# Modulation panels of the feed-forward layers in three places of their own, loaded by GpSimd's queue

## The chip, the cores and the metric

The kernel runs on one core of a Trainium2 chip. Five engines work beside each other, each through its own list of instructions, in order: TensorE (PE in the profile, its weight loads PEld), VectorE (DVE), ScalarE (ACT), GpSimd (POOL) and SyncE (SP), which here issues every DMA. The metric is the device time of one execution in microseconds; the median of three runs of the kernel before is 2368.94 us.

## The reference, cut to what matters

A transformer of two blocks, each of two layers, over 512 tokens of width 1024 in float32. The change touches the two layers of the first block:

```python
c_act = jax.nn.silu(c)
for l in range(DEPTH):                          # 2 layers
    mod = c_act @ ada_w[l] + ada_b[l]           # 1024 -> 6144
    sh1, sc1, g1, sh2, sc2, g2 = split(mod, 6)
    h = x * (1.0 + sc1) + sh1
    y = _even_mixer(h, ...) if l % 2 == 0 else _pool_mixer(h, ...)
    x = _layer_norm(ALPHA * x + g1 * y, ...)
    h = x * (1.0 + sc2) + sh2
    y = _conv_ffn(h, ...)                       # 1024 -> 2 x 2816 -> 1024
    x = _layer_norm(ALPHA * x + g2 * y, ...)
# the second block: mod = silu(c_2) @ ada_w_2[l] + ada_b_2[l], 1024 -> 3072, and the same for c_ctx_2
...
def _conv_ffn(h, w_up, conv_w, conv_b, w_down):
    u, v = jnp.split(h @ w_up, 2, axis=-1)
    ...                                         # causal convolution of width 3 over the tokens of u
    return (jax.nn.silu(uc) * v) @ w_down
```

The modulation vectors are products of one condition vector with a large matrix, so there is much weight to load and little to compute: 96 panels for the first block, and 48 for the second, whose panels serve two condition vectors each.

## The kernel before

**Weights.** A weight panel holds the weights of 128 output columns: 128 partitions by up to 1024 float32. `panel_load` (L342) brings it by DMA into a tile `ws`; `panel_split` turns it into a high part `wh` on ScalarE (L321) and a remainder `wl` on VectorE (L333). TensorE makes three products of a panel and an input that was split in the same way (`mm3`, L356 to L358). In the first block `ws` has four places (`stage=4`) and `wh` and `wl` three each (`panels=3`).

**The feed-forward layer** (`ffn`). It runs in two parts. Each part has 22 up tiles of 24 matmuls each, then 8 down tiles of 33 matmuls each, over the 11 hidden tiles of that part. An up tile that carries u goes through the convolution (a copy with bias on ScalarE, two L981 on VectorE, silu on ScalarE); one that carries v is multiplied in (L987), and the product is split into `gh` (L321) and `gl` (L333), which the down tiles read. A down tile is added to x with its gate (L993 in the first part, L605 in the second).

**Modulation panels.** `ada` makes a list of pieces. A piece loads one panel of 128 rows by 1024 into a `ws` tile (L437) and lets VectorE multiply it with the condition vector, which is held in every partition, and sum along the row (L440): one column of the modulation. For the second block's vectors there are two such instructions for each panel; the first of them writes its product to a scratch tile `ada`. The last piece of a list also loads the bias into a `ws` tile (L444) and adds it (L447). So panels of both kinds take the same four `ws` places in turn, and all loads stand in SyncE's queue.

**When pieces are called.** Lists stand in `self.pending`. `project` calls one piece after each up tile (`background(1)`) and two after each down tile (`bg=DBG`, 2); `flush` calls the rest of a list where its results are needed. In the first feed-forward layer these are list "d" (40 pieces, layer 1) and list "f" (24 pieces with two instructions each, second block); in the second they are "e" (8 pieces) and "g" (24 pieces with two instructions each). The panels of layer 0 are done before the first feed-forward layer.

**Order.** The program text does not fix the order of an engine's instructions. When the program is built, a planner puts them in an order, by its own reckoning of when inputs and places are there; on the chip each engine then keeps that order, and waits where an input is late. `tile(..., tag, bufs)` gives a tile one of `bufs` places in turn; a load waits until the last reader of that place is done. GpSimd has work in the layer norms (`x` in L521), and in the pooling layer between the two feed-forward layers (L1043; L1027 clears pads there).

Of the kernel before, what the change touches and what calls it, by code (L numbers as in the profile page):

```python
# [10 lines left out]
F32 = mybir.dt.float32  # L11
# [6 lines left out]
P = 128  # L18
# [63 lines left out]
def _vector_columns():  # L82
    at, n = {}, 0
    for name, size in _VEC_SIZES:
        at[name] = n
        n += size // P
    return at, n
# [185 lines left out]
class Program:  # L273
    def __init__(self, ctx, tc, I, C, out):
        self.ctx, self.tc, self.nc, self.I, self.C, self.out = ctx, tc, tc.nc, I, C, out
        pool = lambda name, **k: ctx.enter_context(tc.tile_pool(name=name, bufs=1, **k))
        self.keep, self.acts = pool("keep"), pool("acts")
        self.table_users = []
        self.pin(PIN[0])
        self.at, self.nvec = _vector_columns()  # L280
        self.pending = []

    def pools(self, ctx, name, psum, panels=4, stage=4, pk=8):

# [139 lines left out]
    def ada(self, src, cact, bias, dst, tiles, key):  # L424

        nc = self.nc

        class Piece:
            def __init__(self, f):
                self.f, self.key = f, key  # L430

            def __call__(self):
                self.f()

        def piece(m):
            ws = self.wp.tile([P, 1024], F32, tag="ws", name="ws", bufs=self.sbufs)
            nc.sync.dma_start(out=ws, in_=src[m])  # L437
            for i, (c, d) in enumerate(zip(cact, dst)):
                w = self.cp.tile([P, 1024], F32, tag="ada", name="ada") if i < len(dst) - 1 else ws
                nc.vector.scalar_tensor_tensor(out=w, in0=ws, scalar=1.0, in1=c, op0=ALU.mult, op1=ALU.mult, accum_out=d[:, m:m + 1])  # L440

        def close():
            b = self.wp.tile([P, 1024], F32, tag="ws", name="ws", bufs=self.sbufs)
            nc.sync.dma_start(out=b[:, :bias.shape[-1]], in_=bias)  # L444
            for d in dst:
                for a, n in runs:
                    nc.vector.tensor_tensor(out=d[:, a:a + n], in0=d[:, a:a + n], in1=b[:, a:a + n], op=ALU.add)  # L447

        tiles = list(tiles)
        runs = []  # L450
        for m in sorted(tiles):
            if runs and sum(runs[-1]) == m:
                runs[-1] = (runs[-1][0], runs[-1][1] + 1)
            else:
                runs.append((m, 1))
        work = [Piece(lambda m=m: piece(m)) for m in tiles]
        if key == "a":
            return work
        return work[:-1] + [Piece(lambda: (piece(tiles[-1]), close()))]


# [148 lines left out]
    def block1_even(self):  # L610
# [4 lines left out]
        lead, pan = list(range(16, 22)), []  # L615
        pss = [self.psum(("acc0", "sw")[q > 3]) for q in range(6)]
        first = ada(0, [c for m in range(8) for c in (8 + m, m)], "a")
        b = self.keep.tile([P, 48], F32, name="ada_b0")
        with tc.tile_pool(name="e1", bufs=1) as ep:
# [4 lines left out]
            for k in range(KT):  # L624
# [16 lines left out]
                if k == 1:  # L641
                    self.constants()
            self.pending += ada(0, range(16, 24), "b") + ada(0, range(24, 40), "b2") + ada(0, range(40, 48), "c")
            k_lev = self.const("k_levels", ep, I32)
            k_reset = self.const("k_reset", ep)
# [321 lines left out]
    def ffn(self, l, hh, hl, beside=None):  # L967
        nc, tc = self.nc, self.tc
        st = self.stats()
        half = NFF // 2  # L970
        with tc.tile_pool(name=f"ffn{l}", bufs=1) as fp:
            cw = lambda j, f: self.vec("conv_w", (3 * l + j) * NFF + f)
            held, gh, gl = {}, [], []

            def evac(m, ps):
                f = m // 2
                if m % 2 == 0:
                    a = fp.tile([P, T], F32, tag="a", name="a", bufs=2)
                    self.act(a, ps, AF.Identity, scale=cw(2, f), bias=self.vec("conv_b", l * NFF + f))
                    for j in (1, 2):  # L980
                        nc.vector.scalar_tensor_tensor(  # L981
                            out=a[:, j:], in0=ps[:, :T - j], scalar=cw(2 - j, f), in1=a[:, j:], op0=ALU.mult, op1=ALU.add)
                    self.act(a, a, AF.Silu)
                    held[f] = a
                else:
                    a = held.pop(f)
                    nc.vector.tensor_tensor(out=a, in0=ps, in1=a, op=ALU.mult)  # L987
                    for t, g in (("gh", gh), ("gl", gl)):
                        g.append(fp.tile([P, T], F32R, tag=t, name=t, bufs=GBUFS))
                    self.split(gh[-1], gl[-1], a)  # L990

            def first(m, ps):
                nc.vector.scalar_tensor_tensor(out=self.x[:, m, :], in0=ps, scalar=self.mod(l, 5)[:, m:m + 1], in1=self.x[:, m, :],  # L993
                                               op0=ALU.mult, op1=ALU.add)

            def second(m, ps):
                self.residual(st, l, 5, m, ps)
                if m == KT // 2 and beside:
                    beside()

            for part in range(2):
                self.project(self.I[f"up{l}"], list(range(2 * half * part, 2 * half * (part + 1))), KT, [(hh, hl, T)], evac, lead=3 if part == 0 else 1)
                if part == 0:
                    self.flush("c" if l == 0 else "e")
                    self.finish_gate(l, 5)
                self.project(self.I[f"down{l}"], list(range(KT)), half, [(gh, gl, T)], second if part else first, lead=1,
                             k_at=half * part, chunk=(half + 1) // 2, bg=DBG)
                gh.clear()
                gl.clear()
        return st  # L1010


# [68 lines left out]
    def block1_layers(self):  # L1081
        ada = lambda l, ch, key: self.ada(self.I["ada"][l], self.cact[:1], self.I["ada_b"][:, 48 * l:48 * l + 48], [self.mods[l]], ch, key)
        hh, hl = self.block1_even()
        self.pool_share = 0
        self.cond_open()
        self.pending += ada(1, range(40), "d") + self.ada2(0, "f")
        sums = self.ffn(0, hh, hl, self.context)
        self.flush("f")
        hh, hl = self.h_tiles()
        feed = self.context_feed(0, CTX_TILES[0])  # L1090
        self.weave([self.block1_odd(sums, hh, hl)], feed, CRATE[0])
        feed.finish()
        self.pending += ada(1, range(40, 48), "e") + self.ada2(1, "g")
        sums = self.ffn(1, hh, hl)
        self.flush("g")
        return self.between(sums)
# [1113 lines left out]
```

## Time and profile before

| | |
|---|---|
| runs | 2364.86, 2368.94, 2371.18 us (median 2368.94) |
| profiled execution | 2364.25 us, of which the span of the trace is 2362.4 us; granted clock of TensorE 0.976 of full speed |
| PE busy | 2213.0 us, 94% of the span |
| DVE busy | 1632.0 us, 69% |
| ACT busy | 1131.2 us, 48% |
| POOL busy | 354.7 us, 15% |
| DMA | 269.64 MB, all of the kernel's own issues by SP; 37.4% of 16 engines' span |
| L440, both kinds | 192 instructions, 180.2 and 58.7 us busy; DVE idle before them 84.4 and 29.8 us |

The span runs from the first instruction of the trace to the last; the execution's own time has a little more around it. Busy is the time in which an engine works on an instruction; waits and DMA issues are not counted. The first feed-forward layer lies at about 300 to 661 us of the span, the pooling layer after it at about 661 to 760 us, and the second feed-forward layer at about 760 to 1129 us. In rows of the timeline the bracket gives the engine's idle time before the instruction and what ended it; `x3` counts instructions merged into a row. In rows of windows each engine has its busy time and, in brackets, its count of instructions; then stand the granted clock, the busy share of the 16 DMA engines and GB/s.

### The profile page before, as it was taken

Reading aid. Unit: us, or ns where it says so; the run is one execution under the profiler, and the core shown is the slowest. Engines: PE = TensorE matmul, PEld = TensorE weight load, DVE = VectorE, ACT = ScalarE, POOL = GpSimd, SP = SyncE. Lnnn points to the kernel's source line nnn. Section 1 sums busy time; section 2 is a strip of 40 time slices with the busy share of each in tenths; the row PEclk is TensorE's granted clock in tenths of the full one; section 3 lists DMA queues with packets and bytes.
Section 4 is the critical chain, followed back from the end, with each engine's and each line's share of the span. In section 5 each row is a group of like instructions: output and inputs, shape, how many; then the busy total and the mean of one; then the engine's idle time right before and its main releaser. Section 6 shows DMA issues by size and latency. Waiting matters only on the chain.

```text
span 2362.4 us, 39796 instructions
## 1 busy us (share of the span) xinstructions
PE 2213.0 (94%) x15486; PEld 1784.4 (76%) x15486; DVE 1632.0 (69%) x3032; ACT 1131.2 (48%) x2105; POOL 354.7 (15%) x728
## 2 busy tenths in 40 slices
PE   6989989999998999999898999999999999999996
PEld 4667768778775787888686777777787777888885
DVE  6799886578859687444676787787776646555544
ACT  3466453223344332333564565656555445655542
POOL 1321020000002000000103433342423100000001
PEclk9999999999999999999999999999999999999998
DMA  8433456566624656323322222222212432422221
GB/s 285 140 127 125 135 158 194 177 212 195 191 70 139 200 178 205 105 85 97 135 74 60 47 58 53 59 47 60 62 45 46 129 129 92 138 72 72 63 63 45
DMA packets 203933, 269.64 MB, mean 114 GB/s; under 512 B 125408, under 2 KB 137568, under 8 KB 203360
## 3 DMA queue, kind: packets, MB, share of 16 engines
q1 hardware_dynamic: 203744, 267.09, 37.4%
q8 instruction: 122, 2.00, 0.3%
q14 instruction: 67, 0.55, 0.1%
HBM read 250.38 MB, written 16.66 MB: 113 GB/s over the span
## 4 chain that ended last, share of the span: by engine, by line
PE 68%; DVE 15%; DMA 7%; ACT 4%; issue 3%; POOL 2%; SPq 0%; DVEq 0%; ACTq 0%; POOLq 0%
PE acc L358 14%; PE acc L356 14%; PE acc L357 14%; DMA ws<-in_ada_dram 5%; PE c L1751 3%; DVE wl L333 2%; DVE ws L440 2%; PE acc L369 1%; PE sp L1646 1%; PE acc L370 1%; PE sp L1836 1%; PE acc L368 1%; PE misc L1854 1%; PE u L1815 1%; PE u L1646 1%
## 5 line engine op out<-in xcount | busy, mean ns | idle before, releaser
L356 PE MATMUL acc<-hh,wh 128*128 128x512 f32 x1416 | 573.5, 406 | 35.0 <-ACT wh L321 18.3
L358 PE MATMUL acc<-hh,wl 128*128 128x512 f32 x1416 | 570.0, 403 | 11.4 <-DVE wl L333 6.7
L357 PE MATMUL acc<-hl,wh 128*128 128x512 f32 x1416 | 571.4, 404 | 2.0 <-DVE hl L333 1.9
L321 ACT ACTIVATE wh<-ws 128x1024 fp32r<-128x1024 f32 (+3 forms) x307 | 275.5, 901 | 405.9 <-PE acc L357 302.8
L333 DVE TENSOR_TENSOR wl<-ws,wh 128x1024 fp32r<-128x1024 f32 (+4 forms) x294 | 304.8, 1040 | 189.2 <-ACT wh L321 186.5
L356 PEld LDWEIGHTS acc<-hh,wh 128*128 128x128 f32 x1416 | 269.5, 190 | 94.6 <-ACT wh L321 20.1
L358 PEld LDWEIGHTS acc<-hh,wl 128*128 128x128 f32 x1416 | 269.2, 190 | 77.4 <-DVE wl L333 12.4
L357 PEld LDWEIGHTS acc<-hl,wh 128*128 128x128 f32 x1416 | 269.8, 191 | 59.4 <-issue 6.1
L440 DVE SCALAR_TENSOR_TENSOR ws<-ws,cact 128x1024 f32<-128x1024 f32 x144 | 180.2, 1253 | 84.4 <-DMA ws<-in_ada_dram 83.5
L356 PE MATMUL acc<-gh,wh 128*128 128x512 f32 x352 | 138.4, 393 | 4.0 <-ACT gh L321 4.0
L1671 POOL TENSOR_TENSOR sO<-sN,sX 64x15 f32<-64x15 f32 (+2 forms) x270 | 87.3, 323 | 355.8 <-DMA sN<-lt 336.1
L358 PE MATMUL acc<-gh,wl 128*128 128x512 f32 x352 | 138.2, 393 | 1.5 <-DVE wl L333 1.4
L357 PE MATMUL acc<-gl,wh 128*128 128x512 f32 x352 | 138.2, 393 | 0.9 <-DVE gl L333 0.9
L321 ACT ACTIVATE a<-a 128x512 f32<-128x512 f32 x44 | 27.8, 633 | 203.8 <-DVE a L981 203.5
L1672 POOL TENSOR_TENSOR sX<-sX,sO 64x15 f32<-64x15 f32 (+2 forms) x270 | 89.3, 331 | 21.2
L1844 DVE SCALAR_TENSOR_TENSOR S<-sp,gc,gs 64x64 f32<-64x64 f32 x240 | 57.9, 280 | 36.4 <-PE sp L1836 32.7
L2013 POOL TENSOR_TENSOR raw<-raw,k_axial 128x512 f32<-128x512 f32 x16 | 21.9, 1366 | 399.3 <-ACT raw L321 209.7
L356 PEld LDWEIGHTS acc<-gh,wh 128*128 128x128 f32 x352 | 66.5, 189 | 18.9 <-ACT gh L321 5.2
L358 PEld LDWEIGHTS acc<-gh,wl 128*128 128x128 f32 x352 | 66.6, 189 | 16.9 <-DVE wl L333 3.2
L440 DVE SCALAR_TENSOR_TENSOR ada<-ws,cact 128x1024 f32<-128x1024 f32 x48 | 58.7, 1222 | 29.8 <-DMA ws<-in_ada_dram 29.8
L357 PEld LDWEIGHTS acc<-gl,wh 128*128 128x128 f32 x352 | 66.5, 189 | 15.6 <-DVE gl L333 1.9
L356 PE MATMUL acc<-hc,wh 128*128 128x256 f32 x208 | 64.3, 309 | 8.7 <-issue 3.7
(583 smaller groups left out, 4505.3 us busy)
## 6 DMA issues: line engine op xcount, KB each, us to landing
ws<-in_ada_dram SPq DMA_DIRECT2D x144, 512.0 KB, 4.3
ws<-in_up_dram SPq DMA_DIRECT2D x88, 512.0 KB, 4.0
ws<-in_od_in_dram SPq DMA_DIRECT2D x44, 512.0 KB, 3.5
ws<-in_ev_in_dram SPq DMA_DIRECT2D x60, 256.0 KB, 2.9
ws<-in_down_dram SPq DMA_DIRECT2D x32, 384.0 KB, 3.2
ws<-in_w_in_dram SPq DMA_DIRECT2D x22, 512.0 KB, 4.6
ws<-in_down_dram SPq DMA_DIRECT2D x32, 320.0 KB, 3.0
ws<-in_ev_in_dram SPq DMA_DIRECT2D x18, 512.0 KB, 3.6
```

The lines of the kernel that those rows point to most:

```text
L321: ins = self.nc.scalar.activation(out=out, in_=in_, func=func, **k)
L333: (engine or self.nc.vector).tensor_tensor(out=lo, in0=x, in1=hi.bitcast(F32), op=ALU.subtract)
L356: nc.tensor.matmul(ps, wh[:, s], xh, start=start, stop=False)
L357: nc.tensor.matmul(ps, wh[:, s], xl, start=False, stop=False)
L358: nc.tensor.matmul(ps, wl[:, s], xh, start=False, stop=stop)
L368: nc.tensor.matmul(out, xh[:, k, t], wh, start=(k == 0), stop=False)
L440: nc.vector.scalar_tensor_tensor(out=w, in0=ws, scalar=1.0, in1=c, op0=ALU.mult, op1=ALU.mult, accum_out=d[:, m:m + 1])
L1646: nc.tensor.matmul(ps[:, j, :], self.BZ[:, d, h, j, :], st["AR"][d][:, j // 2, i:i + 2, :].rearrange("p s t -> p (s t)"), start=True, stop ...
L1671: pt(out=ob, in0=N[:, :j, j:j + 1].to_broadcast(sh), in1=X[:, j:j + 1, j:].to_broadcast(sh), op=ALU.mult)
L1672: pt(out=X[:, :j, j:], in0=X[:, :j, j:], in1=ob, op=ALU.subtract)
L1751: nc.tensor.matmul(ps[64 * i + r0:64 * i + r0 + m, x, :], lhs(x, i), rhs(x, i), start=True, stop=True)
L1844: nc.vector.scalar_tensor_tensor(out=nxt[H, d, H], in0=sp[H, d], scalar=gd, in1=gs[H, d, H], op0=ALU.mult, op1=ALU.add)
```

## The change

Within `ffn`, from its start to its end, pieces of modulation no longer take `ws` places and SyncE's queue: their panels and biases go to tiles `wa` with three places in the layer's own pool (12 KB more in each partition), and GpSimd's queue issues their loads. That holds for the 96 pieces of lists d, f, e and g and their four biases, 100 loads. Elsewhere `ada_place` is empty and pieces are staged as before.

```diff
-        self.pending = []
+        self.pending, self.ada_place = [], None
...
+        def staged(n, ap):
+
+            pool, tag, bufs, eng = self.ada_place or (self.wp, "ws", self.sbufs, nc.sync)
+            t = pool.tile([P, 1024], F32, tag=tag, name=tag, bufs=bufs)
+            eng.dma_start(out=t[:, :n], in_=ap)
+            return t
+
         def piece(m):
-            ws = self.wp.tile([P, 1024], F32, tag="ws", name="ws", bufs=self.sbufs)
-            nc.sync.dma_start(out=ws, in_=src[m])
+            ws = staged(1024, src[m])
...
         def close():
-            b = self.wp.tile([P, 1024], F32, tag="ws", name="ws", bufs=self.sbufs)
-            nc.sync.dma_start(out=b[:, :bias.shape[-1]], in_=bias)
+            b = staged(bias.shape[-1], bias)
...
     def ffn(self, l, hh, hl, beside=None):
...
             held, gh, gl = {}, [], []
+            self.ada_place = fp, "wa", 3, nc.gpsimd
...
                 gh.clear()
                 gl.clear()
+            self.ada_place = None
         return st
```

## Rows read from the trace of the kernel before

**Rows 1.** The page, part 4: shares of the chain that ended last, by line.
```profile
PE acc L358 14%; PE acc L356 14%; PE acc L357 14%; DMA ws<-in_ada_dram 5%; PE c L1751 3%; DVE wl L333 2%; DVE ws L440 2%; PE acc L369 1%; PE sp L1646 1%; PE acc L370 1%; PE sp L1836 1%; PE acc L368 1%; PE misc L1854 1%; PE u L1815 1%; PE u L1646 1%
```

**Rows 2.** Windows over stretches of both feed-forward layers; columns as told above.
```profile
326.00:434.00 108.00, 107.63 (x476) 88.81 (x475) 72.99 (x100) 39.93 (x52) 0.00 (x0) 1.00 0.62 194
434.00:498.00 64.00, 61.27 (x264) 48.94 (x263) 37.66 (x57) 14.04 (x18) 0.00 (x0) 1.00 0.64 208
498.00:621.00 123.00, 122.34 (x537) 100.03 (x536) 105.22 (x163) 40.34 (x54) 0.00 (x0) 1.00 0.61 192
621.00:661.00 40.00, 37.75 (x159) 30.56 (x158) 27.37 (x44) 15.03 (x25) 0.00 (x0) 0.96 0.57 181
879.00:941.00 62.00, 60.55 (x267) 49.60 (x266) 49.90 (x79) 15.46 (x21) 0.00 (x0) 1.00 0.62 205
941.00:1062.00 121.00, 121.00 (x536) 100.25 (x535) 56.36 (x65) 43.13 (x53) 0.00 (x0) 1.00 0.32 96
```

**Rows 3.** Waits of PE, 330 to 661 us: total, times, longest.
```profile
PE acc L356 <- ACT gh L321: 2.8, 2, 1.9
PE acc L358 <- DVE wl L333: 2.3, 5, 0.9
PE acc L357 <- DVE gl L333: 0.6, 2, 0.3
```

**Rows 4.** Waits of PE, 760 to 1129 us.
```profile
PE acc L356 <- ACT gh L321: 1.2, 1, 1.2
```

**Rows 5.** Groups of DVE, 330 to 661 us: busy, mean ns | idle before.
```profile
L440 DVE SCALAR_TENSOR_TENSOR ws<-ws,cact 128x1024 f32<-128x1024 f32 x61 | 74.6, 1222 | 56.7 <-DMA ws<-in_ada_dram 56.4
...
L440 DVE SCALAR_TENSOR_TENSOR ada<-ws,cact 128x1024 f32<-128x1024 f32 x24 | 29.3, 1222 | 13.4 <-DMA ws<-in_ada_dram 13.4
```

**Rows 6.** Timeline of DVE, 621 to 630 us.
```profile
623.48 1.22 DVE L440 SCALAR_TENSOR_TENSOR ada<-ws,cact 128x1024 f32<-128x1024 f32 x1 [1.33 <-DMA ws<-in_ada_dram]
...
625.90 1.22 DVE L440 SCALAR_TENSOR_TENSOR ada<-ws,cact 128x1024 f32<-128x1024 f32 x1
...
627.04 0.69 DVE L987 TENSOR_TENSOR a<-acc,a 128x512 f32<-128x512 f32 x1
```

**Rows 7.** Timeline of PE, start of the second part's down tiles.
```profile
628.45 0.49 PE L356 MATMUL acc<-gh,wh 128*128 128x512 f32 x1 [1.94 <-ACT gh L321]
...
630.20 0.63 PE L357 MATMUL acc<-gl,wh 128*128 128x512 f32 x1
```

**Rows 8.** Windows: the two stretches with the most DMA.
```profile
0.00:59.00 59.00, 36.66 (x130) 25.90 (x131) 38.84 (x76) 22.10 (x27) 9.46 (x8) 1.00 0.82 285
...
626.00:636.00 10.00, 7.75 (x27) 5.69 (x26) 7.30 (x12) 5.08 (x13) 0.00 (x0) 0.83 0.81 280
```

**Rows 9.** Timeline of SP: the first load of list d.
```profile
295.80 0.33 SPq L437 DMA_DIRECT2D ws<-in_ada_dram  x1
```

**Rows 10.** Groups of POOL, 300 to 761 us.
```profile
L521 POOL TENSOR_SCALAR x<-t,pcol 128x512 f32<-128x512 f32 x16 | 28.9, 1816 | 96.4 <-DVE t L515 95.6 <-ACT cm L321 0.7
...
L1027 POOL MEMSET ph<- 128x16 f32 x4 | 0.2, 111 | 362.8 <-PE acc L358 362.8
```

**Rows 11.** Timeline of DVE after the last piece of list d.
```profile
507.75 0.20 DVE L447 TENSOR_TENSOR mods<-mods,ws 128x40 f32<-128x40 f32 x1
...
508.36 0.16 DVE L1021 TENSOR_TENSOR gs<-mods,pcol 128x8 f32<-128x8 f32 x1
```

**Rows 12.** L440 from 296 to 330 us: ns min/median/max, first and last start.
```profile
L440 DVE SCALAR_TENSOR_TENSOR ws<-ws,cact x3: 1226/1625/1629, 321.4 to 326.8; 128x1024 f32<-128x1024 f32 x3
```

**Rows 13.** DMA issues, 326 to 661 us: count, KB, median us to landing.
```profile
ws<-in_ada_dram SPq DMA_DIRECT2D x61, 512.0 KB, 4.3
...
hh<-in_ctx_dram SPq DMA_DIRECT2D x1, 1024.0 KB, 5.8
```

**Rows 14.** Window over the end of the pooling layer.
```profile
700.00:760.00 60.00, 48.28 (x166) 31.54 (x166) 56.85 (x104) 29.18 (x47) 20.20 (x13) 0.91 0.34 106
```

## The prediction, made before the changed kernel was run

> **What bounds the kernel now.** I read the chain of waits first. It is TensorE's three products of a split panel, 14% each; but 5% of it is VectorE waiting for a modulation panel, and 2% more L440 itself [rows 1]. Part of that lies at the kernel's start, which the change leaves alone, so the second view is windows over the feed-forward layers. TensorE is busy nearly throughout. What it loses is read from the count of matmuls: from 941 to 1062 us, with no piece left to do, 536 in 121 us, 4.43 per us, is its full pace [rows 2]. At that pace the other stretches lack:
>
> 434 to 498 us: 283.5 - 264 = 19.5 matmuls, 4.4 us; 498 to 621: 544.9 - 537, 1.8 us; 621 to 661: 177.2 - 159, 4.1 us; 879 to 941: 274.6 - 267, 1.7 us; 326 to 434: 478.4 - 476, 0.5 us [rows 2].
>
> Together 12.5 us, 0.5% of the time, and no more can be won in these layers. Third, TensorE's waits say who makes the loss: at the start of the down tiles it waits for `gh` and `gl`, and within them for `wl` [rows 3, 4]. All three need VectorE, or what it passes to ScalarE. Fourth, VectorE's groups: it stood idle 56.4 + 13.4 = 69.8 us before pieces whose panel had not landed, with everything behind them in its list held up [rows 5]. An example: before the down tiles of the second part it waits 1.33 us for a panel, then does three L440 in a row, and only then the L987 from which `gh` is made [rows 6]; TensorE stands 1.94 us, and the next matmuls take 0.63 us each [rows 7], where at full pace one starts every 0.23. The granted clock over 626 to 636 us is 0.83, a mix of 2.4 and 1.2 GHz [rows 8]. This is in the 4.1 us above.
>
> **The change part by part.**
>
> *Removed from `ws` and SyncE.* 100 loads go. SyncE pays 0.33 us for an issue [rows 9], 33 us on a queue that carries loads alone; weight panels get all four places instead of sharing them with pieces. Where TensorE waits for `wl`, the wait is VectorE's turn and not a missing weight, so I take 0; below nothing it can't cost, since the same loads are issued earlier, and above it could bring the 0.5 us of the first stretch.
>
> *Added to GpSimd.* 100 issues on an engine that is busy 0.00 us in all six stretches [rows 2]. The trace has no load issued there. Bounds for one: 0.33 us, SyncE's issue, and 1.82 us, GpSimd's own operation on a 128x512 tile [rows 10]; I take 1.0, about the middle, as neither row is nearer. 33 to 182 us lie beside idle time and cost nothing. The cover is gone where L521 runs, in the two layer norms ahead of the feed-forward layers: three places let at most three loads through before a piece has run, so 0 to 5.5 us. I take 0, since GpSimd had long been idle before the first of them (95.6 us for L521 in all) and the three loads need nothing but free memory. The waiting clear of `ph` stands behind the last `gh` reader as before [rows 10].
>
> *Moved: the pace of the pieces.* This decides. Before, a piece could be loaded only when the weight panel ahead of it had taken and freed its place, so pieces went at the pace of TensorE's tiles. With places and a queue of their own they go as fast as VectorE has time. The order on VectorE is the planner's, and the trace shows that it runs free work far ahead of where the text has it: the last sum of list d is followed in under a microsecond by the pooling layer's gate at 508 us, which the text has after the whole feed-forward layer [rows 11]. It also shows that pieces come last among what is ready: the first panel of list d was issued at 295.80 us, but its piece ran at 321.4 us, after nearly the whole layer norm [rows 9, 12].
>
> VectorE's own work without pieces is 56.36 of 121 us, 0.466 [rows 2], so 0.534 is free. A piece of list d then takes 1.222 / 0.534 = 2.29 us in the planner's order, 40 take 92 us; a piece of list f twice that, 24 take 110 us. Both lists would be done at about 326 + 202 = 528 us, before the down tiles of the second part. Gains: 4.1 us after 621, 1.2 of the 1.8 us before that (a third of the stretch is still in list f), 3.0 of 4.4 us at 434 to 498 (list f is under way, and one block of 1.2 us can still stand ahead of an L987), and 1.7 us in the second layer, whose 56 instructions start as early: 10.0 us.
>
> *What is late next: the loads of list d.* 0.524 MB in 2.29 us is 229 GB/s, with the weights' 96 [rows 2] 325. The highest that a long stretch shows is 285 GB/s at a share of 0.82; ten busy microseconds show 280 [rows 8]. So landing will be that of a full DMA: 5.8 us, the context's load among others, rather than the pieces' 4.3 [rows 13]. One turn of a place: issue 1.0, landing 5.8, piece 1.22, together 8.0 us, a third of it 2.67 us. That is 0.38 us per piece more than VectorE's order has room for, 15 us over 40 pieces. TensorE doesn't feel it until its lead is used up: three places for `wh` and `wl` are two tiles ahead, 48 matmuls, 10.8 us [rows 2]. So 15 - 10.8 = 4.2 us, with jitter 5 us are given back. Bounds: issue 0.33 with landing 4.3 make a turn of 5.85 us, within VectorE's 6.87, and give back 0; issue 1.82 with landing 5.8 make 8.84, 2.95 a piece, 26 - 10.8 = 15.6 us. List f has twice the time and is safe at either end.
>
> One page of the Trainium skill prices this lower. "DMA: Bandwidth & Descriptors", section "Specifications", gives about 1 us to the first byte for a load issued from GpSimd and 0.6 us from SyncE; an estimate from that page is 0.4 us on the landing, a turn of 0.33 + 4.7 + 1.22 = 6.25 us, nothing given back, and 10 us gained. No row shows such a load.
>
> *Sum.* -10.0 + 5.0 = -5.0 us on the profiled execution's 2364.25 us, 2359.3. That execution lies 4.7 us below the median of the runs shown, 2368.94; on the median's scale I forecast 2364.
>
> **The rivals.**
>
> *All of it is won.* Either the loads land as before (turn under 6.9 us) or the pieces keep the program's pace, one per tile, and a turn has 16 us. Nothing is given back, and list f's blocks don't meet a change of part: -12 us, 2357. For it: 4.3 us is the median while two loads are in flight, and a third place covers it. Against it: the early run of free work [rows 11].
>
> *VectorE stands behind slow loads (slower).* Place: the first feed-forward layer, 326 to about 450 us, list d. Each piece in VectorE's list holds the splits of weights behind it; a slow turn sets the pace of three tiles. Its point: the loss passes 10 us when a piece takes more than 2.29 + (10 + 10.8) / 40 = 2.81 us, a turn of 8.4, issue and landing of 7.2 us together. At 8.3 us a piece takes 3.17, the lag is 35, TensorE loses 24.5 and the net is +15: 2384; at 10 us it is +37. What could make loads that slow is VectorE holding off GpSimd while it writes out a transfer. For it: beside L521, an L440 took 1625 ns in place of 1222, so the two engines do hold each other up [rows 5, 12]; and VectorE would be full in this stretch. Against it: L521 works through a whole tile, and no row shows what an issue occupies.
>
> The skill's page "SBUF — State Buffer", section "Who interferes with whom", says that VectorE's two-port modes (copy, cast, `tensor_scalar`) shut GpSimd out of writing, while an instruction with two SBUF inputs contends only with one that reads. VectorE's work in these layers is of the second kind; so by that page this rival is unlikely, and the slowed L440 beside a reading L521 agrees with it (1625 against 1222 ns).
>
> *Nothing to be had.* The waits at the change of parts come from blocks of L440 more than from late panels: in the example 1.33 us of waiting stand ahead of L987, and three L440 of 1.2 us [rows 6]. If the planner keeps putting blocks there, the time stays, 2369, within 3 us either way. Against it: there would be no pieces left there.
>
> The pooling layer could also suffer: list e may run into it, where VectorE is busy 56.85 of 60 us [rows 14]. Three early pieces would cost 3.7 us at most. They came last in the layer norm before [rows 9, 12], so I put this into the range.
>
> **How the numbers follow.** A difference of 0.3%, 7 us, is what can be told from none. Forecast (-10 to +1, centre -5): 0.40, of which 0.12 lie beyond -7. All won: 0.22. Slower: 0.29. Nothing: 0.09. Faster is 0.12 + 0.22 = 0.34, with a little of the others' noise 0.35; slower 0.29 with as much 0.30; the same 0.35. The forecast's own range is 2358 to 2370; all cases to 8 in 10 are 2354 to 2390, which leaves out the worst third of the slower rival and a few per cent below.
>
> **What would show it.** Right: pieces done before 560 us; waits of VectorE for modulation panels few after list d; no PE wait over 1 us at 628 us and the granted clock 1.00 there; 536 matmuls per 121 us from list d's end on; issues on GpSimd of about 1 us, landing near 6 us while list d runs. Wrong: L440 still in pairs up to 640 us (the planner did not run ahead); VectorE waiting 3 us before each third L440 with PE waiting for `wl` in 326 to 450 us (the slower rival); or loads from GpSimd landing in over 7 us.

## The result, and the profile of the changed kernel

The changed kernel took 2378.97 us (median of 8 runs, 2371.39 to 2383.27), the kernel before 2365.69 us beside it (8 runs, 2360.73 to 2371.18): a ratio of 1.0055, 95% interval 1.0036 to 1.0074. It is slower, by some 13 us. Timed again later it gave 1.0037 (1.0022 to 1.0052). The time lies inside the range that I gave for all cases to 8 in 10 (2354 to 2390 us), outside the forecast's own (2358 to 2370); the direction was forecast wrong.

Most of what I had named as signs of success is there. First the six windows of [rows 2], in the changed kernel's trace, and one of list d without its start:

```profile
326.00:434.00 108.00, 104.05 (x448) 84.48 (x447) 92.63 (x141) 36.78 (x47) 23.55 (x44) 0.98 0.85 284
434.00:498.00 64.00, 60.94 (x259) 48.95 (x258) 63.02 (x109) 15.46 (x21) 9.54 (x18) 0.97 0.76 238
498.00:621.00 123.00, 123.00 (x544) 101.84 (x543) 71.12 (x93) 42.98 (x53) 2.13 (x4) 1.00 0.38 121
621.00:661.00 40.00, 40.00 (x178) 33.13 (x177) 18.33 (x25) 16.05 (x26) 0.00 (x0) 1.00 0.38 112
879.00:941.00 62.00, 62.00 (x276) 51.32 (x275) 35.15 (x52) 16.30 (x22) 2.13 (x4) 1.00 0.39 109
941.00:1062.00 121.00, 121.00 (x536) 100.19 (x535) 54.83 (x63) 41.65 (x51) 0.00 (x0) 1.00 0.33 102
...
340.00:426.00 86.00, 86.00 (x378) 70.79 (x376) 75.18 (x113) 26.77 (x34) 18.56 (x35) 0.99 0.88 297
```

From 498 us on TensorE runs at its full pace in each of these stretches, and the stall at 628 us with its low clock is gone. The losses stand in the first two rows: 448 matmuls where 476 ran before, 259 where 264 did. TensorE's waits say for whom (first the stretch of [rows 3], then, from 760 us, that of [rows 4]; total, times, longest):

```profile
PE acc L356 <- DVE a L987: 3.4, 1, 3.4
PE acc L358 <- DVE wl L333: 3.2, 4, 2.0
PE acc L357 <- DVE gl L333: 0.3, 1, 0.3
...
PE acc L358 <- DVE wl L333: 4.6, 2, 2.7
...
```

The line numbers have moved: the piece's product is now L446, the convolution L987 (L981 before) and the product with v L993 (L987 before). The wait for the convolution is new, and so is most of the wait for `wl` in the second layer (0.9 us before). VectorE itself idles less before pieces, 14.0 + 0.9 = 14.9 us against 69.8 [rows 5]:

```profile
L446 DVE SCALAR_TENSOR_TENSOR wa<-wa,cact 128x1024 f32<-128x1024 f32 x64 | 77.6, 1221 | 14.1 <-DMA wa<-in_ada_dram 14.0
...
L446 DVE SCALAR_TENSOR_TENSOR ada<-wa,cact 128x1024 f32<-128x1024 f32 x24 | 29.3, 1222 | 0.9 <-DMA wa<-in_ada_dram 0.9
```

In the place of [rows 10] and [rows 13], GpSimd's issues take 0.53 us each and their loads 4.8 us to land:

```profile
L439 POOL DMA_DIRECT2D wa<-in_ada_dram x64 | 34.1, 534 | 145.8 <-DVE wa L446 143.5 <-DVE mods L452 2.0 <-POOL x L526 0.3
```
```profile
wa<-in_ada_dram POOLq DMA_DIRECT2D x64, 512.0 KB, 4.8
```

Where the few idle microseconds of VectorE lie is what matters. GpSimd's timeline at the start of the first layer, after the layer norm's last operation (L526, L521 before):

```profile
319.63 6.12 POOL L526 TENSOR_SCALAR x<-t,pcol 128x512 f32<-128x512 f32 x3 [1.31 <-DVE t L520]
326.07 1.81 POOL L439 DMA_DIRECT2D wa<-in_ada_dram  x3 [0.31 <-POOL x L526]
```

Before, SyncE had issued list d's first load at 295.80 us [rows 9]. VectorE's timeline after that:

```profile
325.74 0.69 DVE L333 TENSOR_TENSOR hl<-lnh,hh 128x512 fp32r<-128x512 f32 x1 [0.62 <-ACT hh L321]
330.11 1.22 DVE L446 SCALAR_TENSOR_TENSOR wa<-wa,cact 128x1024 f32<-128x1024 f32 x1 [3.68 <-DMA wa<-in_ada_dram]
...
332.90 1.22 DVE L446 SCALAR_TENSOR_TENSOR wa<-wa,cact 128x1024 f32<-128x1024 f32 x1 [0.40 <-DMA wa<-in_ada_dram]
...
334.05 2.71 DVE L987 SCALAR_TENSOR_TENSOR a<-acc,pcol,a 128x511 f32<-128x511 f32 x4
336.68 1.21 DVE L333 TENSOR_TENSOR wl<-ws,wh 128x1024 fp32r<-128x1024 f32 x1
...
770.07 1.23 DVE L446 SCALAR_TENSOR_TENSOR wa<-wa,cact 128x1024 f32<-128x1024 f32 x1 [3.18 <-DMA wa<-in_ada_dram]
...
784.10 1.23 DVE L446 SCALAR_TENSOR_TENSOR wa<-wa,cact 128x1024 f32<-128x1024 f32 x1 [3.00 <-DMA wa<-in_ada_dram]
...
792.01 1.23 DVE L446 SCALAR_TENSOR_TENSOR ada<-wa,cact 128x1024 f32<-128x1024 f32 x1 [2.55 <-DMA wa<-in_ada_dram]
...
795.83 1.22 DVE L333 TENSOR_TENSOR wl<-ws,wh 128x1024 fp32r<-128x1024 f32 x1
```

It waits 3.68 us for a modulation panel, does three products, and only then the four L987 that read TensorE's accumulators, and the next `wl`. In the second layer products of lists e and g stand ahead of a `wl` in the same way, with waits of 3.0 and 2.55 us. TensorE, whose work is behind both:

```profile
332.44 0.39 PE L357 MATMUL acc<-hl,wh 128*128 128x512 f32 x1
336.25 0.47 PE L356 MATMUL acc<-hh,wh 128*128 128x512 f32 x1 [3.43 <-DVE a L987]
...
797.10 0.50 PE L358 MATMUL acc<-hh,wl 128*128 128x512 f32 x1 [2.70 <-DVE wl L333]
```

A stall costs more than its own length here. After the wait of 3.43 us the granted clock is low for some 4 us, a mix of its two levels of 2.4 and 1.2 GHz (the same columns as above):

```profile
338.00:342.00 4.00, 4.00 (x11) 3.17 (x12) 4.00 (x5) 0.63 (x1) 0.00 (x0) 0.57 0.72 173
```

By 342 us TensorE is 5.4 us behind the kernel before, counted from the layer's first matmul: waits of 3.43 and 0.34 us, and for the rest matmuls at the lower clock.

**A table by stage.** The clearest account comes from the same matmuls in two traces. In the trace of before the stages begin and end at these starts of matmuls: A, up tiles of part 0, 308.65 to 433.74 us; B, down tiles of part 0, to 497.85; C, up tiles of part 1, to 619.54; D, down tiles of part 1, to 687.10; F, up tiles of part 0 in the second layer, 766.25 to 888.37; G, its down tiles, to 950.01; the second layer ends at 1129.53. (The first layer thus runs to 687 us, not to about 661 as I had written.) Each cell is how much longer a stage took than before (us); "layers" is the sum from 308.65 to 1129.53, "rest" what came between there and the end. Pooling layer and second part of the second layer differ by 0.1 us or less, except in e14.

| kernel | ratio, 95% | A | B | C | D | F | G | layers | rest |
|---|---|---|---|---|---|---|---|---|---|
| changed | 1.0055 (1.0036, 1.0074) | 7.2 | 0.3 | -1.8 | -4.4 | 7.9 | -2.0 | 7.2 | 9.3 |
| e10 changed, again | 1.0037 (1.0022, 1.0052) | 7.7 | 0.3 | -1.8 | -4.4 | 10.4 | -2.0 | 10.2 | 6.4 |
| e1 places, SyncE | 0.9970 (0.9952, 0.9988) | 1.1 | -0.8 | -1.8 | -4.4 | 1.5 | -2.0 | -6.5 | 6.0 |
| e2 queue alone | 1.0088 (1.0060, 1.0116) | 0.4 | 5.6 | 4.9 | 4.9 | 2.5 | 4.2 | 22.5 | 4.2 |
| e4 second layer only | 1.0036 (1.0020, 1.0053) | -0.1 | 0.9 | 0.0 | 0.2 | 11.2 | -2.0 | 10.2 | 7.6 |
| e5 changed, one hold | 1.0011 (0.9995, 1.0027) | 0.0 | 0.2 | -1.8 | -4.4 | 4.4 | -2.0 | -3.6 | 13.4 |
| e6 first six by SyncE | 0.9968 (0.9949, 0.9987) | 1.4 | 1.7 | -1.8 | -4.4 | -0.1 | -2.0 | -5.3 | 6.7 |
| e7 first six by GpSimd | 0.9986 (0.9972, 1.0000) | 4.6 | -3.7 | -1.8 | -4.4 | 5.5 | -2.0 | -1.9 | 3.5 |
| e8 places, SyncE, one hold | 0.9949 (0.9933, 0.9965) | 0.0 | 0.8 | -1.8 | -4.4 | 2.5 | -2.0 | -5.0 | 3.9 |
| e13 the same again | 0.9962 (0.9946, 0.9978) | -0.1 | -0.1 | -1.8 | -4.4 | -0.1 | -2.0 | -8.5 | 7.1 |
| e9 two places, SyncE | 0.9991 (0.9976, 1.0005) | -0.1 | 4.7 | -1.8 | -4.4 | 1.3 | -2.0 | -2.2 | 1.1 |
| e11 e5, first three share | 1.0000 (0.9986, 1.0013) | 1.7 | 2.6 | -1.8 | -4.4 | 3.6 | -2.0 | -0.3 | 6.7 |
| e12 places, SyncE, two holds | 0.9950 (0.9929, 0.9971) | 0.0 | -4.5 | -1.8 | -4.4 | 0.5 | -2.0 | -12.2 | 5.3 |
| e17 the same again | 0.9941 (0.9921, 0.9960) | 0.0 | -4.5 | -1.8 | -4.4 | 0.4 | -2.0 | -12.3 | 4.4 |
| e14 e5, one place in layer 2 | 1.0058 (1.0037, 1.0079) | 0.0 | 1.2 | -1.8 | -4.4 | 3.3 | 8.2 | 9.4 | 10.8 |
| e15 two holds, GpSimd | 1.0010 (0.9994, 1.0026) | 0.1 | 2.7 | -0.9 | -4.4 | 4.8 | -2.0 | 0.2 | 7.9 |
| e16 two holds, shared places | 0.9986 (0.9969, 1.0002) | 0.0 | -2.7 | 0.8 | 1.2 | -0.2 | -2.0 | -2.9 | 9.5 |

"Rest" is positive in all 17, the fastest too, with a median of 6.7 us. So the one profiled execution of before was most likely short there by about as much, and that part is not the change's; there is no second trace of before to show it. The column "layers" follows the ratios: it lies within 2.3 us of what the ratio makes of the time before in 13 kernels, and 4 to 7 us off in the changed kernel's first trace, e5, e8 and e14.

### The profile page after: what moved, and what is told of

Same layout as the page of the kernel before. It is cut to its first block, busy times and chain, and to the rows that moved or that the text cites. A ratio compares the mean times of both kernels' runs of the same rounds, so it can differ in the third digit from the quotient of the medians.

```text
span 2381.5 us, 39856 instructions
## 1 busy us (share of the span) xinstructions
PE 2220.1 (93%) x15486; PEld 1787.4 (75%) x15486; DVE 1631.0 (68%) x3032; ACT 1135.6 (48%) x2105; POOL 409.2 (17%) x828
## 4 chain that ended last, share of the span: by engine, by line
PE 68%; DVE 12%; DMA 6%; issue 6%; POOL 4%; ACT 4%; SPq 1%; POOLq 0%; DVEq 0%; ACTq 0%
PE acc L356 14%; PE acc L358 14%; PE acc L357 14%; PE c L1758 3%; DMA ws<-in_ada_dram 1%; PE sp L1653 1%; PE acc L369 1%; PE acc L370 1%; PE acc L368 1%; PE sp L1843 1%; PE u L1653 1%; PE misc L1861 1%; PE u L1822 1%; DVE ws L446 1%; PE misc L1592 1%
## 5 line engine op out<-in xcount | busy, mean ns | idle before, releaser
L446 DVE SCALAR_TENSOR_TENSOR wa<-wa,cact 128x1024 f32<-128x1024 f32 x96 | 116.5, 1221 | 21.9 <-DMA wa<-in_ada_dram 21.4
L439 POOL DMA_DIRECT2D wa<-in_ada_dram x96 | 51.2, 533 | 249.8 <-DVE wa L446 246.5
L446 DVE SCALAR_TENSOR_TENSOR ws<-ws,cact 128x1024 f32<-128x1024 f32 x48 | 64.4, 1349 | 16.5 <-DMA ws<-in_ada_dram 15.0
```

The source lines that it names most:

```text
L439: eng.dma_start(out=t[:, :n], in_=ap)
```

## The experiments

Each run is compared with the kernel before on the same chip.

**Places or queue?** Theory A: the loss is at the start of the layers, for reasons of order and memory; rival B: it is GpSimd's queue. e1 keeps the places and gives the loads back to SyncE; e2 keeps the queue and gives the places back.

```diff
-            self.ada_place = fp, "wa", 3, nc.gpsimd
+            self.ada_place = fp, "wa", 3, nc.sync                          # e1
+            self.ada_place = self.wp, "ws", self.sbufs, nc.gpsimd          # e2
```

> Own places as in the change, but the loads in SyncE's queue as before. Theory A (the time is lost where each feed-forward layer begins: the places lie in the layer's pool, so the first three loads go out only when the layer norm lets its memory go, and VectorE has their three products ahead of the next weight splits; the queue is not the cause): the starts of both layers keep their stalls, about 2375 to 2382 us, with TensorE standing 3 us or more near 336 us and again between 770 and 800 us. Theory B (GpSimd's queue is the cause: issue behind the layer norm's scale-and-shift on that engine, slow landing): 2362 to 2368 us and no such stalls.

> The shared places as before, but the loads issued by GpSimd in the feed-forward layers. Theory A: the pieces keep the pace of the shared places and two of the first loads can go before the layer norm, so the start of the layers costs little: 2362 to 2369 us, the stall near 336 us under 1.5 us. Theory B: 2374 to 2382 us, with the landing of the loads at 4.5 us or more and VectorE waiting for them at both starts.

Measured 0.9970 and 1.0088: theory A as I put it is refuted. Places alone gain, and GpSimd's queue costs with the new places as with the old. By what way it costs is not said by this, since the planner writes another order when the queue is another. TensorE's waits in e1, 325 to 345 and then 755 to 800 us:

```profile
PE acc L358 <- DVE wl L333: 1.5, 1, 1.5
...
PE acc L358 <- DVE wl L333: 1.6, 3, 0.8
...
```

The memory part of A holds, though: in e1 too the first three loads leave together when the layer norm ends, at 323.16, 323.54 and 324.01 us. SyncE's queue waits there, from 300 to 330 us, for an operation of the layer norm on GpSimd, which shares nothing with the panel but memory:

```profile
SPq L439 <- POOL x L526: 0.7, 1, 0.7
```

The late loads cost little in e1 because the written order differs: `wl` stands right behind the three products instead of behind four L987. e2 loses nothing at the start of the first layer and then something in each stage. VectorE's idle time before pieces, 330 to 661 us, is 62.2 + 25.2 = 87.4 us there, against 69.8 [rows 5]; what each stage pays for is not taken apart further:

```profile
L446 DVE SCALAR_TENSOR_TENSOR ws<-ws,cact 128x1024 f32<-128x1024 f32 x61 | 74.6, 1223 | 62.7 <-DMA ws<-in_ada_dram 62.2
L446 DVE SCALAR_TENSOR_TENSOR ada<-ws,cact 128x1024 f32<-128x1024 f32 x24 | 29.4, 1224 | 25.3 <-DMA ws<-in_ada_dram 25.2
```

**Which layer, and the order.** e4 makes the change in the second layer alone. e5 leaves places and queue as changed, starts the pieces after the layer's third group of up tiles, and puts their products behind that group's split in VectorE's order ("one hold").

```diff
+            self.ada_place = (fp, "wa", 3, nc.gpsimd) if l else None       # e4
```
```diff
# e5; self.hold = 3 where a layer begins, split() keeps its subtraction in self.last
                 pan = [first.pop(0) if first else self.panel(src[m], k_at + k0, kn) for m in tl]
+                self.hold -= 1
+                self.behind = self.last if self.hold == 0 else self.behind
...
-            self.background(bg)
+            self.hold > 0 or self.background(bg)
...
+                if self.behind: self.tc.add_manual_dep(s.ins, self.behind.ins.name, NOSYNC)   # s: the product, L446
```

> The change in the second feed-forward layer alone; the first one as before. Theory A: the second layer's start costs about 8 us and about 2 us come back in it: 2369 to 2374 us; the first layer's part of the loss (5 us at its start, 5 us at the change of part, 9 us regained after) is gone with its gains. If the layers are not where the time goes (a shift of everything after), the time stays at 2376 to 2382 us with the second layer unchanged.

> The change whole (places and queue), but the first piece of each feed-forward layer follows the layer's third group of up tiles in the program, and its products stand behind that group's weight split in VectorE's order. Theory A: the stalls at both starts go (5 and 8 us) and the gains inside the layers stay: 2362 to 2368 us, no stall of TensorE over 1.5 us in 330 to 345 us or 765 to 800 us. Rival D (the weight panels themselves land late beside the new loads, 8 us instead of 4): the stalls stay, 2374 to 2380 us. Rival of a shift that has nothing to do with the layers: 2372 us or more although both starts are clean.

e4: 1.0036, more than I expected; F costs 11.2. e5: 1.0011; the order alone takes A from 7.2 to 0.0 with loads as late as in the changed kernel (first issue 323.27 us), so the late loads cost what they did through VectorE's written order. In F 4.4 us stay. Its ratio is some 6 us above what its stages say; that stays open. TensorE's waits in e5, 755 to 800 us:

```profile
PE acc L356 <- ACT wh L321: 3.9, 1, 3.9
PE acc L358 <- DVE wl L333: 0.4, 1, 0.4
```

It waits for `wh` now, the split of a weight panel that landed at 764.51 us, 8.07 us after its issue, and no longer for VectorE.

> The changed kernel once more, for a second profile and a second set of times beside the variants. If the loss is of the written order and the start of the layers, it repeats in place and size: about 5 us near 332 to 345 us, 3 to 4 us at the change of part (430 to 455 us), 8 us between 760 and 800 us, and about 10 us regained; ratio 1.002 to 1.006. Shifts before 296 us and after 1130 us that don't repeat are the run's own.

The changed kernel repeats stage by stage, F with 10.4 us; its +2.5 us before 296 us did not repeat.

**Which loads?** Own places; e6 issues the first six loads of a layer by SyncE and the others by GpSimd, e7 the reverse.

```diff
-            pool, tag, bufs, eng = self.ada_place or (self.wp, "ws", self.sbufs, nc.sync)
+            pool, tag, bufs, eng = self.ada_place and self.ada_place.pop() or (self.wp, "ws", self.sbufs, nc.sync)
...
+            self.ada_place = [(fp, "wa", 3, nc.gpsimd)] * 64 + [(fp, "wa", 3, nc.sync)] * 6   # e6; e7: engines exchanged
```

> Own places; the first six loads of each feed-forward layer go out by SyncE, the others by GpSimd. If the queue's price falls at the start of the layers (three loads let go at once there, out of step with SyncE's weight panels, and the written order laid out for later panels): both starts as with SyncE's queue alone (about 1 us each) and only the change of part in the first layer still costs 2 to 4 us: a ratio to before of 0.997 to 1.000, some 2361 to 2369 us. If every load by GpSimd costs its share (0.29 us from release to issue where SyncE needs 0.03, 96 loads): 1.003 to 1.006, 2374 us or more.

> The reverse: own places; the first six loads of each feed-forward layer by GpSimd, the others by SyncE. If the price is at the starts: TensorE stands 3 us or more near 336 us and 5 us or more in sum in 765 to 800 us, ratio 1.001 to 1.005. If the price is spread over all loads by GpSimd: ratio 0.996 to 0.999, as with SyncE's queue alone.

e6: 0.9968, the same as with SyncE alone (0.9970). Six of 66 loads in the first layer and six of 34 in the second carry nearly the whole price of the queue (and of the order that is written with it). e7: 0.9986, below the 1.001 I expected: the stalls at both starts are there, 3.2 us for L987 and 4.7 us for `wl`, and A and F cost 4.6 and 5.5 us, but B gains 3.7 us.

**Contention at the second layer's start.** Rival D: the three loads that GpSimd lets go at once slow the weight panels. Landing of what was issued from 757 to 768 us before, and from 763 to 768 us in the changed kernel (count, KB, median us):

```profile
ws<-in_up_dram SPq DMA_DIRECT2D x3, 512.0 KB, 4.5
ws<-in_ada_dram SPq DMA_DIRECT2D x2, 512.0 KB, 4.8
c_save<-cm SPq DMA_DIRECT2D x5, 128.0 KB, 2.9
```
```profile
ws<-in_up_dram SPq DMA_DIRECT2D x3, 512.0 KB, 8.0
wa<-in_ada_dram POOLq DMA_DIRECT2D x3, 512.0 KB, 7.2
c_save<-cm SPq DMA_DIRECT2D x3, 128.0 KB, 6.8
```

e11 is e5 with the first three pieces in one place, so that one load goes out at a time; e14 is e5 with a single place in the second layer.

```diff
+            self.ada_place = [(fp, "wb", 1, nc.gpsimd)] * 3 + [(fp, "wa", 2, nc.gpsimd), (fp, "wa", 2, nc.gpsimd), (fp, "wb", 1, nc.gpsimd)] * 22   # e11, taken with pop(0)
+            self.ada_place = fp, "wa", 1 if l else 3, nc.gpsimd                                                    # e14
```

> Three places and GpSimd's queue, with the first products behind the third group's weight split, and in addition the first three loads of each layer share one place, so that one goes out at a layer's start and not three at once. If the 4 us that the second layer's start still lost when only the order was mended (TensorE standing 4.3 us at 765.6 us for an up panel that took 8 us to land) are contention of the three loads with the weight panels and stores: that stall falls under 1.5 us, up panels there land in 4 to 6 us, ratio 0.996 to 0.9995. If not: the stall of 4 us stays, ratio 1.000 to 1.002.

> GpSimd's queue and own places, first products behind the third group's weight split, but one place alone in the second feed-forward layer, so that at its start one load is under way and not three. Contention: TensorE's stall of 4.3 us near 765 us falls under 1.5 us and the up panels issued there land in 4 to 6 us instead of 8. Not contention: a stall of 3 us or more stays there although one load alone is under way. The later pieces of that layer then turn at 6 to 8 us each (32 loads, some 220 us of the layer's 370); the time is 0.997 to 1.000 by contention.

e11 (1.0000) decides nothing: the order written for GpSimd drew two later loads ahead into the other places, so three went out all the same, the panels took 6.8 us and the wait for `wh` 3.0. e14 does what was meant. Waits of TensorE, 755 to 800 us, and landings, 752 to 758 us:

```profile
PE acc L356 <- ACT wh L321: 1.1, 1, 1.1
PE acc L358 <- DVE wl L333: 0.9, 2, 0.5
```
```profile
ws<-in_up_dram SPq DMA_DIRECT2D x3, 512.0 KB, 5.2
c_save<-cm SPq DMA_DIRECT2D x4, 128.0 KB, 4.8
wa<-in_ada_dram POOLq DMA_DIRECT2D x1, 512.0 KB, 6.0
```

One load in place of three: the panels land in 5.2 us instead of e5's 8.1, the wait falls from 3.9 to 1.1 us (both expectations have 4.3 us; e5's trace shows 3.9). VectorE's order is the same in e5 and e14 over this stretch, so that is contention. The time, 1.0058, misses my 0.997 to 1.000: one place is too slow for the rest of the layer (F falls by 1.1 us alone, G costs 8.2, and 3.0 us more come after it).

Contention with what, with a second queue or with three loads at once? e8 (below) is e5 with the loads in SyncE's queue, and from 750 to 788 us VectorE's order is the same. Landings, 753 to 759 us:

```profile
ws<-in_up_dram SPq DMA_DIRECT2D x2, 512.0 KB, 5.5
wa<-in_ada_dram SPq DMA_DIRECT2D x1, 512.0 KB, 3.9
```

With one load ahead the panels take 5.5 us by one queue and 5.2 by two. What SyncE's queue did was to let one load go and keep the second, which left at 765.67 us, behind up panels that were issued as their places came free; GpSimd's queue let three go at 753.66, 754.26 and 754.78 us (e5). So the number of loads let go ahead of the panels is shown to cost, and a second queue only in that it lets them go. While they were under way they had most of the DMA engines' time. In the changed kernel, from 767 to 771 us (q0 is GpSimd's queue, q1 SyncE's; packets, MB, share of 16 engines):

```profile
q0 software_dynamic: 364, 1.36, 89.4%
q1 hardware_dynamic: 161, 0.17, 11.7%
```

**How many places?**

```diff
+            self.ada_place = fp, "wa", 2, nc.sync                          # e9
```

> Two places instead of three, SyncE's queue. A place turns in some 6.5 us (landing 5.3 and a product of 1.2), so two give 3.3 us a piece: list d ends near 460 us instead of 430 and list f still ends before 630 us. If the gain is the separation of places, not their number: ratio 0.996 to 0.999 as with three. If running far ahead is what pays: 0.999 to 1.002, and VectorE waits for loads between 345 and 460 us with weight splits behind.

0.9991: the low edge of the one expectation and the high edge of the other. Two places give C, D and G in full but cost 4.7 us in B; whether that is the number of places is not shown, since the written order changed as well.

**A version that beats both.** e8 is e5 with SyncE's queue; e13 repeats it. e12 adds a second hold; e17 repeats it. e15 is e12 by GpSimd, e16 is e12 with the shared places.

```diff
             if part == 0:
-                    self.flush("c" if l == 0 else "e")
+                    self.flush("c" if l == 0 else "e"); self.behind = self.last    # e12: behind the part's last gl
```
```diff
+            self.ada_place, self.hold = (fp, "wa", 3, nc.sync), 3                           # e8, e12
+            self.ada_place, self.hold = (fp, "wa", 3, nc.gpsimd), 3                         # e15
+            self.ada_place, self.hold = (self.wp, "ws", self.sbufs, nc.sync), 3             # e16
```

> Own places, SyncE's queue, and the first pieces of each layer held behind the third group's weight split. If the stalls left at the starts (1.9 us near 332 us, some 4 us in sum in 760 to 785 us) come from the products standing ahead of the splits: 2 to 4 us less than with places and SyncE's queue alone, ratio 0.995 to 0.9965. If they come from late weight panels: no change from it, 0.997.

> Own places, SyncE's queue and the first products behind the third group's weight split, once more, to tell it from places and SyncE's queue alone: 0.994 to 0.9965 if the hold is worth some us, 0.9965 to 0.9985 if its first timing was luck (the sums of stalls in the two traces differ by less than 1 us).

> Own places, SyncE's queue, first products behind the third group's weight split, and all products that the program issues after the first part's up tiles also behind the last gl split of that part. If what is lost at the change of part (TensorE standing 3.3 us at 442.8 us) comes from products crowding VectorE ahead of gh and gl: 2 to 3 us less than without, ratio 0.9935 to 0.995. If the products crowd the down tiles instead: stalls of 2 us or more for a weight split between 445 and 508 us and 0.995 to 0.998.

> The fastest version once more: own places, SyncE's queue, both holds. Its feed-forward layers were 12 us shorter in the trace than before; ratio 0.993 to 0.997 if that repeats.

> The order of the fastest version (first products behind the third group's weight split, later ones behind the first part's last gl split) with three own places, by GpSimd's queue. If the queue costs only where loads go out beside the weight panels at the layers' starts: the first layer as with SyncE's queue, the second layer's start 4 us worse: ratio 0.996 to 0.998. If the queue has no cost once the order is mended: 0.994 to 0.996. If GpSimd's loads cost throughout: 0.999 or more.

> The same order with the shared places and SyncE's queue as before the change. If the gain comes from places of their own: 0.998 to 1.003 (the pieces keep the pace of the shared places and the stall at 628 us is there). If the mended order alone gains: 0.995 to 0.997.

e8 and e13, 0.9949 and 0.9962: below e1, with intervals that overlap e1's; stages of the same kernel differ by 2.6 us in F between the two traces, so a gain of the one hold over e1 is likely but not shown. e12 and e17, 0.9950 and 0.9941: the second hold turns B from +0.8 and -0.1 to -4.5 in both. Windows of e12:

```profile
326.00:434.00 108.00, 107.62 (x475) 88.81 (x474) 74.89 (x102) 43.11 (x55) 0.00 (x0) 1.00 0.56 185
434.00:498.00 64.00, 64.00 (x284) 52.98 (x283) 52.25 (x90) 14.26 (x17) 0.00 (x0) 1.00 0.88 296
```

284 matmuls where before had 264 and full pace is 283.5. Of the 12.5 us that these layers lacked, 12.2 are won. e15 is 1.0010, worse than the 0.996 to 0.998 I expected: beside F's 4.8 us, B loses 2.7. Its down panels issued from 455 to 478 us land later than e12's (e12's row for the same stretch first, e15's second), but they are not what is waited for. TensorE waits for `wl` (433 to 500 us; e12 has no wait there), and ScalarE, which splits the panels first, waits for TensorE, once for VectorE and never for a panel (440 to 500 us):

```profile
ws<-in_down_dram SPq DMA_DIRECT2D x3, 320.0 KB, 3.8
```
```profile
ws<-in_down_dram SPq DMA_DIRECT2D x3, 320.0 KB, 6.2
...
PE acc L358 <- DVE wl L333: 4.9, 3, 2.4
...
ACT wh L321 <- PE acc L357: 45.2, 13, 6.9
```

The `wl` stand behind products whose own panels are late (VectorE waits 2.31 us for one at 472.85 us, TensorE 2.38 us at 476.93 us). VectorE's order also differs between e12 and e15 in this stage, so how much of B is the queue and how much the order stays open. e16, 0.9986: its layers are 2.9 us shorter by the order without the places, where the places without the order gave 6.5 (e1) and both 12.2.

## Why the prediction was wrong

- *What bounds, and how much can be won:* right. 12.5 us lacking; the best version wins 12.2.
- *The gains:* three of four terms came as sized. Forecast 4.1 at the second change of part, measured 4.4 (D); 1.2, measured 1.8 (C); 1.7 in the second layer, measured 2.0 (G). The fourth, 3.0 at the first change of part, did not come (B, +0.3): products of list f filled VectorE there (63.02 of 64 us busy; list d had ended at 432 us) and stood ahead of `wl`. e12 gets this term in full by holding them back. 8.2 of 10.0 us were gained, less 0.3 in B.
- *SyncE and `ws`:* taken as 0. What the removal gave was hidden by what follows; e1 gives no sign against it.
- *The pace of list d:* size right, consequence not. A piece took 2.56 us (330.11 to the bias add at 432.39 us, 40 pieces), forecast 2.67. That it agrees is partly luck: an issue took 0.53 us (taken as 1.0, bounds 0.33 and 1.82) and landing 4.8 us (taken as 5.8, from a load twice as large), so by the prediction's own sum a turn of a place is 6.6 us, 2.2 a piece, less than was measured. And little of the 5 us to be given back in this list by a lead running out was lost there: from 340 to 426 us TensorE was busy for 86.00 of 86 us, with the DMA engines at a share of 0.88. The last tiles of A, to 443 us, lose 1.8 us to `wl` behind products of lists d and f; e5, whose pieces of list d take 2.40 us each, loses none there.
- *The failed step* is the start of the layers: "I take 0, since GpSimd had long been idle before the first of them ... and the three loads need nothing but free memory." The memory is the point: the places lie in the layer's own pool, on memory that the layer norm holds to its end, so the loads left at 326.07 us where one had left at 295.80 before, and VectorE, whose order put three products first, waited 3.68 us with L987 and `wl` behind. The 95.6 us of idle time lay ahead of the layer norms' own operations, while that memory was still in use. The term 0 (bounds 0 to 5.5, for another reason) measured 5.4 us by 342 us and 7.2 over stage A, of which the hold removes all; in the second layer 7.9 to 10.4 (F). With these, -7.9 + 15.1 = +7.2 us in the layers, in place of -10 + 5.
- *In the second layer* a second term was missing. I asked how slow the new loads would be, not how slow they make the weight panels: 8.0 us in place of 4.5. About 3 us of F are this (at that wait e5 falls 3.5 us behind, e14 0.6); with the order mended F is 4.4 (e5), so 3.5 to 6 us are the order. The Trainium skill, "DMA: Bandwidth & Descriptors", section "Queues, rings and completion order", says that each DMA engine takes turns, packet by packet, between the queues that have work. The trace agrees that the urgent queue does not go first, but the turns were not equal shares: 1.36 MB for GpSimd's queue and 0.17 for SyncE's from 767 to 771 us, with two up panels and two stores of SyncE's queue still to land.
- *The slower rival* had the direction, and VectorE standing behind slow loads is its mechanism; its place (all of list d), its price (+15) and its point (2.81 us a piece) were not it: 2.56 us was not over it, and nearly all of the loss came from the first loads, as e6 shows. Its cause, VectorE holding off GpSimd's issues, shows nowhere: they took 530 to 746 ns, 96 of them, 533 on average.
- *Signs:* of the five that I called right three showed as told, full pace came at 498 us and not at list d's end (259 matmuls from 434 to 498 us), and the last had lower numbers. Two that I called wrong showed as well, at the starts alone: VectorE waiting over 3 us with TensorE behind, and loads landing in over 7 us (7.2, second layer). Signs of the gain say nothing of what is paid elsewhere.
- The ratios ask for 5 to 17 us, the layers show 7 to 10; what lies beyond in the first trace (2.5 us ahead of 296 us, 9.3 after 1130 us) either did not repeat or is there in faster kernels as well.

The 0.4 us more to the first byte for a load from GpSimd, on the same page of the Trainium skill, section "Specifications", can't be told from the traffic here. With own places the loads took 4.7 us by GpSimd (changed kernel) and 4.5 by SyncE (e1) in the median of all 96, but 4.9 and 5.3 from 340 to 430 us. It was not what decided.

## What to carry to other kernels

Splitting a background stream off into places of its own can pay; giving it a queue of its own as well took away the one thing that ranked it behind the urgent loads: three loads went out ahead of the panels at the second layer's start, where the shared queue had let one go. When a load moves to a new buffer, ask which pool's memory it lies on and when that comes free, and look at the first few loads apart from the steady pace: six of each layer's loads carried nearly all of the loss here. And where work runs ahead freely, hold it behind the few instructions that the bottleneck is waiting for; on top of the places that order was worth nearly as much as they were (5.7 us in the layers after 6.5), and 2.9 us without them.

## What the runs showed of the hardware

- A load by GpSimd begins 0.29 us after the product that frees its place and occupies the engine 0.53 us; by SyncE 0.03 and 0.33 us (medians, 340 to 430 us, 36 loads of the changed kernel and 37 of e1, of which 31 had a product to wait for).
- With three loads of 512 KB from a second queue beside them, loads of the same size took 8.0 instead of 4.5 us to land and stores of 128 KB 6.8 instead of 2.9 us; with one beside them, 5.2 and 4.8 us from a second queue (e14), 5.5 us for the loads from the same one (e8).
- After a wait of 3.43 us TensorE's granted clock was 0.57 from 338 to 342 us; of the 5.4 us lost by then, some 1.7 are this, an estimate from 4 us at 0.57.
- Stages C, D and G differ from before by the same -1.8, -4.4 and -2.0 us in all the kernels whose pieces are done by then, to within 0.02 us, while the time after 1130 us varies by 12 us from one execution to another.
